# Attention scores in a hybrid decoder step: from two full-array products per head to three half-array products per head

## The chip, the cores and the metric

The kernel runs on one core of one Trainium2 chip. The metric is the device time of one execution in microseconds, given as the median of several runs. A profiled execution beside them gives the trace: every instruction on TensorE (PE; its weight loads are listed apart as PEld), VectorE (DVE), ScalarE (ACT), GpSimd (POOL) and the SyncE queue (SP) that issues the DMAs.

## The reference, cut to what matters

One layer of a hybrid decoder: 2048 prompt tokens and 8 sampled tokens, model width 1024. The input is normalised and projected into one wide vector whose columns feed three branches: attention with dilated windows, a gated linear recurrence, and cross-attention to a memory. The branches are gated, projected, merged and projected once more. The change touches the prompt's attention alone:

```python
A_WINDOWS = (128, 512, 2048)
A_DILATIONS = (1, 4, 16)
A_GROUPS = 3
A_HEADS = 8
A_HEAD_DIM = 64
...
    s = jnp.einsum('brnqhd,brnkhd->brnhqk', qb, kb) * (Dh ** -0.5)
...
    s = jnp.where(mask[None, None, :, None], s, -jnp.inf)
    m = jnp.max(s, axis=-1, keepdims=True)
    p = jnp.exp(s - m)
    l = jnp.sum(p, axis=-1, keepdims=True)
    o = jnp.einsum('brnhqk,brnkhd->brnqhd', p / l, vb)
    lse = (m + jnp.log(l))[..., 0].transpose(0, 1, 2, 4, 3)
```

There are three groups of eight heads of width 64. In each group the tokens are split into residue classes of the dilation, and 128 queries at a time read their own block of 128 keys and the block before it, where there is one. The result is wanted at nearly fp32 accuracy.

## The kernel before, in words

**Exact halves.** To keep nearly fp32 accuracy the kernel multiplies in the type float32r and splits each factor into a high part (a cast to float32r) and a low part (the rest). A product is then made of several products of parts. The projections use three: high by high, high by low, low by high (lines 402 to 404, and 163 to 165 elsewhere).

**Order of work.** TensorE's instructions keep the order in which the program issues them. A loop at the end of the kernel's second phase writes this order: `gate_stream` is the main stream (the last 24 units of the input projection, lines 402 to 404), and beside it run side streams. A side stream yields an estimated cost on TensorE and the least time until it is due again; when its time has come by this planned clock its next piece is issued, else the next piece of the projection. For the attention the gap is 3.0 us (`ATT_GAP`), and a step's scores are planned at 0.86 us. These numbers are the same before and after. While one attention step's results travel through the other engines, TensorE works on the projection. When the attention has ended, the recurrence follows as the next side stream, then the memory attention and the sampled tokens. The other engines' instructions are put in order by the framework, which also places the semaphores. The data's DMAs of this stretch are issued on the SP queue in turn.

**The attention stream** (`attention`) takes 96 steps: 4 pairs of heads, 3 groups, 8 segments of 256 queries. Three stages are in flight. One turn of the stream issues the weighted values of the step two back (line 611; evicted at line 614), the transposes of the weights of the step before (line 595; evicted at line 597), and the scores of the current step.

A step's scores cover two blocks (`b`) of 128 queries and two heads (`h`). A block has 256 key columns where there is a block before it, else 128; group 2 has only single blocks. Per block and head, VectorE adds the mask and takes the minimum of the negated scores (line 580), and ScalarE takes the exponential and its sum (line 582).

**The split before.** Queries of both heads are loaded twice, by two DMAs, so that each head's 64 dimensions lie on both halves of the 128 partitions (line 526; the key is loaded at line 528). VectorE casts the queries (`qh`, line 540, 512 columns), and makes per head a tile `km` whose one half holds the high part of the keys and whose other half holds the low part (lines 544 and 545, 64 partitions each, twice per step), then the low part of the queries (`ql`, line 546, 512 columns). With the contraction over 128 partitions, `qh` by `km` gives high by high plus high by low, and `ql` by `km` gives low by high plus low by low: two products per block and head (lines 575 and 576), eight in a step. `km` keeps the keys of two steps, for the block before.

**Banks.** The attention has five banks of the accumulator (PSUM): two for scores (one per block, holding both heads), two for transposes, one for values. The projection has three others.

**Merge.** When a pair of heads has finished its three groups, `merge` combines them by their sums; its work on VectorE (lines 693, 696, 700) and GpSimd (line 695) and its DMAs run during the next pair's steps. The gated projections' evictions (lines 479 to 497) use the same engines.

Of the kernel before, what the change touches and what calls it, by code (L numbers as in the profile page):

```python
# [10 lines left out]
F32 = mybir.dt.float32  # L11
F32R = mybir.dt.float32r
AF = mybir.ActivationFunctionType
ALU = mybir.AluOpType
# [29 lines left out]
class Region:  # L44
    """Rings of buffers, by tag, in parts (tile, from, to: KB) of on-chip tiles; what reuses a buffer waits for its last users only."""
# [23 lines left out]
class Banks:  # L69
    """Rings of PSUM banks, by tag."""  # L70
# [27 lines left out]
def tile_hybrid_step(ctx: ExitStack, tc: tile.TileContext, I: dict, O: dict):  # L98
# [68 lines left out]
    # ================= normalised inputs and the input projection =================  # L167
# [9 lines left out]
    def at_token(t0):  # L177
        """Chunk that holds the 128-token tile (or the sampled tokens) at t0, and its columns there."""
        i = max(i for i, (c0, _) in enumerate(CHUNKS) if c0 <= t0)
        return i, t0 - CHUNKS[i][0]  # L180

    class Weights:
        """A unit of 256 weight columns, brought in by pieces of 256 rows as exact high and low parts."""
# [24 lines left out]
    if True:  # L208
# [12 lines left out]
        class Prep:  # L221
            """Normalised columns c0.. of src as exact high and low parts."""
# [41 lines left out]
        class Values:  # L264
            """A unit of w_v: the values of the sampled tokens beside its weights, then the prompt's by token tile."""
# [119 lines left out]
    class Projector:  # L385
        """Feature-major products of the units of w_t; the weights of the next unit are prepared half a unit ahead."""
# [29 lines left out]
    # forget-gate lower bound: softmax over the depth axis, first row  # L416
# [45 lines left out]
    # order of the last 24 units of w_t: az, bq, bf, bz, cq, cz (2 each), merge gates (12)  # L462
# [38 lines left out]
    def until(u):  # L501
        """Nothing before the given unit of the gate stream has begun."""
        while progress[0] < u:
            yield 0.0, 1.0

    # Side streams yield (time on the tensor engine of what they issued, least time until their next issue).
    def attention(ap, pool, rnd8, spawn):
        """Unnormalised outputs to uT, minimum of -s/8 and sum to st [p, g, (m l), h, 16]; three stages in flight.
# [915 lines left out]
```

## Time and profile before

| | |
|---|---|
| time, median of 3 runs | 3179.41 us (3178.95 to 3179.91) |
| profiled execution, span from first to last instruction | 3169.3 us |
| attention's stretch (990 to 1675 us) | 685 us for 96 steps |
| TensorE busy in that stretch | 644.51 us |
| VectorE busy in that stretch | 491.91 us |
| ScalarE busy in that stretch | 349.32 us |

No time other than its span is listed for the profiled execution. In the rows of the trace a matmul's duration is modelled and overlaps the next one's, so a stream's pace is read from start to start. "Idle before" is the time in which the engine stood still just before the instruction, and the name behind the arrow is what ended it. "SPq" is the queue that issues DMAs. An instruction group is named by its line in the kernel, its engine, and the tiles it writes and reads.

### The profile page before, as it was taken

To read this page: it belongs to the slowest core of one execution; us is meant where nothing else is said; L and a number is where in the kernel's file an instruction comes from. 1 tells how busy PE (TensorE), PEld (TensorE's weight loads), DVE (VectorE), ACT (ScalarE), POOL (GpSimd) and SP (SyncE) were. 2 spreads that over 40 slices of the span, in tenths; PEclk is the share of its full clock that TensorE was granted. 3 is DMA by queue.
4 is the path that set the end of the run, shared out by engine and by line. 5 is a ranking of instruction groups with operands and counts; after the bars stand their busy time and mean duration, and the time that the engine had idled before them with its cause. 6 is when DMAs were issued, how large, how long until landed. Compare 5 with 4: busy or idle time off the path is not lost. (4 is left out here: it accounts for less than half of the span.)

```text
span 3169.3 us, 56318 instructions
## 1 busy us (share of the span) xinstructions
PE 3023.6 (95%) x21644; PEld 2768.5 (87%) x21644; DVE 1530.8 (48%) x3827; ACT 993.0 (31%) x2468; POOL 1021.2 (32%) x836
## 2 busy tenths in 40 slices
PE   6999999999999999999989999999998988999998
PEld 6999999999999987878878888888886778899986
DVE  8700002222224776777772277777757356233232
ACT  4412110000003654434552244444443433201222
POOL 4312126556663211111222231112125125634411
PEclk9999999999999999999989999999999999999999
DMA  4332222112123567767675323233246467665442
GB/s 137 103 97 88 72 78 75 68 67 80 67 80 111 134 168 188 170 170 191 166 170 153 108 88 97 84 99 98 89 127 180 116 164 216 199 175 176 156 146 95
DMA packets 383134, 400.11 MB, mean 126 GB/s; under 512 B 89416, under 2 KB 306120, under 8 KB 379536
## 3 DMA queue, kind: packets, MB, share of 16 engines
q1 hardware_dynamic: 382864, 396.50, 43.3%
q8 instruction: 170, 2.79, 0.4%
q14 instruction: 100, 0.82, 0.1%
HBM read 257.71 MB, written 138.67 MB: 125 GB/s over the span
## 5 line engine op out<-in xcount | busy, mean ns | idle before, releaser
L402 PE MATMUL bank<-rnd 128*128 128x384 f32 (+2 forms) x2880 | 1033.8, 359 | 13.8 <-ACT side L479 7.6
L404 PE MATMUL bank<-rnd 128*128 128x384 f32 (+2 forms) x2880 | 1010.1, 351 | 6.4 <-POOL rnd L201 6.4
L403 PE MATMUL bank<-rnd 128*128 128x384 f32 (+2 forms) x2880 | 1010.2, 351 | 0.0
L402 PEld LDWEIGHTS bank<-rnd 128*128 128x128 f32 x2880 | 550.3, 191 | 43.3 <-ACT side L479 7.9
L404 PEld LDWEIGHTS bank<-rnd 128*128 128x128 f32 x2880 | 548.3, 190 | 32.2 <-POOL rnd L201 7.6
L403 PEld LDWEIGHTS bank<-rnd 128*128 128x128 f32 x2880 | 549.6, 191 | 23.3 <-issue 1.9
L163 PE MATMUL bank<-rnd 128*128 128x256 f32 (+4 forms) x1648 | 532.4, 323 | 8.4 <-DVE raw L1249 4.2
L165 PE MATMUL bank<-rnd 128*128 128x256 f32 (+4 forms) x1648 | 529.2, 321 | 3.5 <-POOL rnd L248 3.4
L164 PE MATMUL bank<-rnd 128*128 128x256 f32 (+4 forms) x1648 | 529.5, 321 | 1.9 <-POOL rnd L1228 1.2
L201 POOL TENSOR_TENSOR rnd<-raw,rnd 128x512 fp32r<-128x512 f32 x172 | 227.7, 1331 | 557.2 <-ACT rnd L200 550.9
L163 PEld LDWEIGHTS bank<-rnd 128*128 128x128 f32 (+1 forms) x1648 | 313.4, 190 | 25.2 <-ACT rnd L1214 3.6
L165 PEld LDWEIGHTS bank<-rnd 128*128 128x128 f32 (+1 forms) x1648 | 313.4, 190 | 17.3 <-POOL rnd L248 4.6
L164 PEld LDWEIGHTS bank<-rnd 128*128 128x128 f32 (+1 forms) x1648 | 313.6, 190 | 15.4 <-POOL rnd L1228 1.5
L200 ACT CAST rnd<-raw 128x512 fp32r<-128x512 f32 x172 | 105.4, 618 | 647.5 <-PE bank L403 449.3
L450 DVE TENSOR_TENSOR raw<-bank,raw 128x384 f32<-128x384 f32 (+2 forms) x120 | 70.4, 586 | 444.1 <-POOL side L455 179.3
L582 ACT ACTIVATE raw<-raw 128x256 f32<-128x256 f32 (+1 forms) x384 | 173.2, 453 | 157.4 <-DVE raw L580 156.5
L695 POOL TENSOR_TENSOR side<-side 128x512 f32<-128x512 f32 x32 | 51.6, 1614 | 334.5 <-DMA side<-stC 271.1
L1249 DVE TENSOR_TENSOR raw<-raw,bank 128x412 f32<-128x412 f32 (+1 forms) x120 | 67.3, 580 | 169.2 <-PE bank L165 93.7
L495 ACT ACTIVATE side<-side 128x384 f32<-128x384 f32 (+2 forms) x120 | 65.4, 545 | 241.1 <-DVE side L494 235.0
L491 POOL TENSOR_TENSOR side<-side 128x384 f32<-128x384 f32 (+2 forms) x60 | 67.8, 1129 | 226.7 <-ACT side L490 205.4
L580 DVE CUSTOM_DVE_ANT_0 raw<-bank,c_amask 128x256 f32<-128x256 f32 (+1 forms) x384 | 119.6, 358 | 18.0 <-PE bank L576 8.3
L286 DVE COPY raw<-bank 8x64 f32<-8x64 f32 x32 | 7.0, 220 | 246.3 <-PE bank L281 245.5
(267 smaller groups left out, 4260.8 us busy)
## 6 DMA issues: line engine op xcount, KB each, us to landing
raw<-in_w_t SPq DMA_DIRECT2D x144, 256.0 KB
raw<-qT SPq DMA_DIRECT2D x192, 128.0 KB
raw<-sgT SPq DMA_DIRECT2D x96, 206.0 KB
sgT<-side SPq DMA_DIRECT2D x72, 192.0 KB
qT<-side SPq DMA_DIRECT2D x12, 1028.0 KB
out_kT<-side SPq DMA_DIRECT2D x12, 1028.0 KB
out_vN<-raw SPq DMA_DIRECT2D x96, 128.0 KB
raw<-out_vN SPq DMA_DIRECT2D x96, 128.0 KB
```

The lines of the kernel that those rows point to most:

```text
L163: T.matmul(out, lhsT=lh, rhs=rh, start=(i == 0), stop=False)
L164: T.matmul(out, lhsT=lh, rhs=rl, start=False, stop=False)
L165: T.matmul(out, lhsT=ll, rhs=rh, start=False, stop=(i == n - 1))
L200: A.copy(hi, raw)
L201: G.tensor_tensor(lo, raw, hi.bitcast(F32), op=ALU.subtract)
L402: T.matmul(ps[:, :w], lhsT=hi, rhs=xh[c][:, k, :], start=(k == 0), stop=False)
L403: T.matmul(ps[:, :w], lhsT=hi, rhs=xl[c][:, k, :], start=False, stop=False)
L404: T.matmul(ps[:, :w], lhsT=lo, rhs=xh[c][:, k, :], start=False, stop=(k == KT - 1))
L450: V.tensor_tensor(t1[:, :w], ps[:, :w], rc[:, c0:c0 + w], op=ALU.mult)
L491: G.tensor_tensor(ow, ow, ew, op=ALU.mult)
L580: V.tensor_tensor_reduce(sm[:, :w], s[:, h, :w], amask[:, m0:m0 + w], -0.125, 1.0e38, ALU.add, ALU.min, accum_out=nmc)
L582: A.activation(sm[:, :w], sm[:, :w], AF.Exp, scale=-1.0, bias=nmc, accum_out=sts[hp][:, g, 1, h, idx:idx + 1])
```

## The change

Queries are loaded once, by one DMA, with the two heads on the two halves of the partitions as the keys have them. Queries and keys are each split into a high and a low tile of 128 partitions by 256 columns, by four VectorE instructions in place of six. Per block and head the scores are three products over that head's 64 partitions only: high by high, high by low, low by high; low by low is left out. The heads alternate within each product, and each head has a bank of its own that holds both blocks, in place of a bank per block that holds both heads. All twelve products of a step are issued ahead of the minima. The text of comments is taken out as well, which leaves the line numbers nearly as they were.

```diff
-        qh = rnd8.tile([128, 2, 256], F32R, name="a_qh")
-        ql = rnd8.tile([128, 2, 256], F32R, name="a_ql")
-        km = rnd8.tile([128, 2, 4, 128], F32R, name="a_km")
+        qh = rnd8.tile([128, 256], F32R, name="a_qh")
+        ql = rnd8.tile([128, 256], F32R, name="a_ql")
+        kh = rnd8.tile([128, 4, 128], F32R, name="a_kh")
+        kl = rnd8.tile([128, 4, 128], F32R, name="a_kl")
...
-            q = pool.tile([128, 2, 256], F32, tag="q", name="a_q")
-            for half in range(2):
-                dma(q[64 * half:64 * half + 64], qT[g * 4 + hp].rearrange("(h d) t -> d h t", h=2)[:, :, pp])
+            q = pool.tile([128, 256], F32, tag="q", name="a_q")
+            dma(q, qT[g * 4 + hp, :, pp])
...
             V.tensor_copy(qh, q)
             kv = k.rearrange("p (b t) -> p b t", b=2)
-            for h in range(2):
-                hi, lo = slice(64 * h, 64 * h + 64), slice(64 - 64 * h, 128 - 64 * h)
-                V.tensor_copy(km[hi, h, sl, :], kv[hi])
-                V.tensor_tensor(km[lo, h, sl, :], kv[hi], km[hi, h, sl, :].bitcast(F32), op=ALU.subtract)
+            V.tensor_copy(kh[:, sl, :], kv)
+            V.tensor_tensor(kl[:, sl, :], kv, kh[:, sl, :].bitcast(F32), op=ALU.subtract)
             V.tensor_tensor(ql, q, qh.bitcast(F32), op=ALU.subtract)
...
-            out = []
+            out, todo = [], []
+            ss = [ap.tile([128, 2, 256], F32, tag=f"s{h}", name="a_s") for h in range(2)]
             for b in range(2):
...
-                s = ap.tile([128, 2, 256], F32, tag="s", name="a_s", bufs=2)
+                bb = slice(b * 128, b * 128 + 128)
+                for j, (x, y) in enumerate(((qh, kh), (qh, kl), (ql, kh))):
+                    for h in range(2):
+                        hr = slice(64 * h, 64 * h + 64)
+                        T.matmul(ss[h][:, b, :w].rearrange("p (b t) -> p b t", t=128), lhsT=x[hr, bb], rhs=y[hr, ks, :],
+                                 start=(j == 0), stop=(j == 2))
+                todo.append((b, idx, blocks, w, m0))
+            for b, idx, blocks, w, m0 in todo:
                 sms = []
-                for h in range(2):
-                    o = s[:, h, :w].rearrange("p (b t) -> p b t", t=128)
-                    bb = slice(b * 128, b * 128 + 128)
-                    T.matmul(o, lhsT=qh[:, h, bb], rhs=km[:, h, ks, :], start=True, stop=False)
-                    T.matmul(o, lhsT=ql[:, h, bb], rhs=km[:, h, ks, :], start=False, stop=True)
                 for h in range(2):
...
-                    V.tensor_tensor_reduce(sm[:, :w], s[:, h, :w], amask[:, m0:m0 + w], -0.125, 1.0e38,
+                    V.tensor_tensor_reduce(sm[:, :w], ss[h][:, b, :w], amask[:, m0:m0 + w], -0.125, 1.0e38,
                                            ALU.add, ALU.min, accum_out=nmc)
```

## The prediction

> **What bounds the kernel now.** I read the page first, then the table of stretches, the waits of the attention's stretch, and the order of time on TensorE.
>
> ```profile
> span 3169.3 us, 56318 instructions
> PE 3023.6 (95%) x21644; PEld 2768.5 (87%) x21644; DVE 1530.8 (48%) x3827; ACT 993.0 (31%) x2468; POOL 1021.2 (32%) x836
> PE   6999999999999999999989999999998988999998
> ```
>
> TensorE (PE) is busy in nearly every slice: the kernel is one long stream of matmuls in an order fixed beforehand. A microsecond taken out of that stream, or out of a stall in it, moves all that comes behind; one taken from another engine counts only where TensorE waits. The profiled execution's span is 3169.3 us, and the median of the runs is 3179.41: 10.1 us lie around the span, and I carry them over unchanged.
>
> ```profile
> core 0: us, PE busy (x) PEld busy (x) DVE busy (x) ACT busy (x) POOL busy (x), PEclk, DMA share, GB/s
> 990.00:1675.00 685.00, 644.51 (x4434) 565.53 (x4433) 491.91 (x1586) 349.32 (x1126) 125.81 (x94) 0.97 0.65 167
> ```
>
> The attention's 96 steps lie in this stretch, 685/96 = 7.1 us each. TensorE stands idle for 685.00 - 644.51 = 40.5 us, and its granted clock is 0.97, which costs up to 0.03 x 685 = 21 us more. VectorE (DVE) is at 491.91/685 = 72%.
>
> ```profile
> ACT raw L582 <- DVE raw L580: 156.5, 81, 6.5
> PEld bank L595 <- ACT raw L582: 38.8, 81, 4.1
> DVE r L544 <- DMA raw<-out_kT: 25.3, 7, 7.0
> PE bank L595 <- ACT raw L582: 17.9, 20, 3.9
> PEld bank L576 <- DVE r L546: 10.9, 16, 2.9
> PE bank L576 <- DVE r L546: 8.2, 14, 2.7
> PEld bank L575 <- DVE r L545: 7.2, 17, 1.5
> PE bank L575 <- DVE r L545: 3.4, 4, 1.3
> PE bank L611 <- ACT raw L597: 4.1, 4, 2.1
> ```
>
> (Columns: total us, times, longest.) Two waits hold TensorE. The score products (L575, L576) wait for VectorE's split of q and k: 3.4 + 8.2 = 11.6 us by the matmul rows, 7.2 + 10.9 = 18.1 by the weight loads. The transposes (L595) wait for the exponentials, 17.9 us by the matmuls, 38.8 by the loads, and those wait for VectorE's masked minimum (L580, 156.5 us). Both waits lead to VectorE.
>
> **The score products.** Now eight full matmuls a step, each with a 128-column weight load; then twelve of 64 rows, in pairs on the two halves of the rows.
>
> ```profile
> 1516.66 0.28 PE L576 MATMUL bank<-r 128*128 128x256 f32 x1
> ...
> 1517.49 0.34 PE L402 MATMUL bank<-rnd 128*128 128x384 f32 x1
> ```
> ```profile
> 1492.32 0.28 PE L576 MATMUL bank<-r 128*128 128x128 f32 x1
> ...
> 1493.10 0.45 PE L402 MATMUL bank<-rnd 128*128 128x512 f32 x1
> ```
> ```profile
> L575 PE MATMUL bank<-r 128*128 128x256 f32 x216 | 61.5, 313 | 1.5 <-DVE r L545 1.3
> L575 PE MATMUL bank<-r 128*128 128x128 f32 x168 | 45.4, 300 | 2.8 <-DVE r L545 2.1
> ```
>
> Durations overlap, so I count pitch, start to start. Seven products of 256 columns take 0.83 us, 0.119 each; seven of 128 columns 0.78 us, 0.111 each. L576 runs as often as L575, so now 432 x 0.119 + 336 x 0.111 = 88.7 us. There are 108 wide and 84 narrow blocks, with three pairs each. If a pair takes the pitch of one matmul: 324 x 0.119 + 252 x 0.111 = 66.5 us, 22.2 less. If the twelve follow one another: 133.0 us, 44.3 more. Half the columns cost almost the same pitch, so the weight load sets it, and the question is whether the two heads' loads run side by side. No row has 64-row operands; the nearest ones split the array by columns:
>
> ```profile
> 1813.39 0.76 PE L757 MATMUL bank<-raw 128*32 128x32 f32 x64
> 1814.08 0.44 PE L402 MATMUL bank<-rnd 128*128 128x384 f32 x1
> ```
> ```profile
> 1836.09 0.34 PE L404 MATMUL bank<-rnd 128*128 128x384 f32 x1
> 1836.35 0.68 PE L788 MATMUL bank<-raw 128*64 128x64 f32 x8
> 1836.96 0.44 PE L402 MATMUL bank<-rnd 128*128 128x384 f32 x1
> 1837.24 0.34 PE L403 MATMUL bank<-rnd 128*128 128x384 f32 x1
> 1837.42 0.34 PE L404 MATMUL bank<-rnd 128*128 128x384 f32 x1
> ```
>
> L757 goes round four column strips: 64 products with their loads in 0.69 us, 0.011 each. L788 stays on one strip: eight in 0.61 us, 0.076 each, with twice the columns. So strips compute and load side by side, and I take the pair at one pitch, -22.2 us; the other end is +44.3.
>
> The Trainium skill, "TensorE: Matmul & The Clock Gate", section "LDWEIGHTS (loading the stationary operand)", speaks against the change: a load takes about its columns over 1.2 GHz whatever its rows, an estimated 107 ns for 128 columns, so half the rows save nothing; the 0.111 pitch agrees. By that figure 1152 loads in place of 768 add 41 us if they queue.
>
> **Going in and out of the half-array.** L404 to L788 takes 0.26 us where 0.18 is usual (L403 to L404): 0.08 to empty the array. Behind the strips L402 to L403 takes 0.28: 0.10 because the first load had no matmul to hide behind. I count 0.18 to 0.20 for each passage, so 0.2 us into the scores (from the transposes, full-array today) and 0.2 out: 0.4 x 96 = 38.4 us. The lower end is nothing, if halving rows is no passage; a gain has no ground. I take 38.4, since the column strips show it. Where the scores wait for VectorE anyway, part hides under that wait.
>
> The Trainium skill, "TensorEngine Tiling (Array Packing)", section "Key Properties", says that a change of tiling mode drains TensorE; the 0.26 agrees, for column strips, and no row here shows it for rows; by that rule the rival without passages falls away.
>
> Pairs and passages make +16.2 us in TensorE's stream.
>
> **The split on VectorE.**
>
> ```profile
> L545 DVE TENSOR_TENSOR r<-raw,r 64x256 fp32r<-64x256 f32 x192 | 91.5, 476 | 5.9
> L546 DVE TENSOR_TENSOR r<-raw,r 128x512 fp32r<-128x512 f32 x96 | 70.1, 730 | 2.0
> L544 DVE CAST r<-raw 64x256 fp32r<-64x256 f32 x192 | 66.3, 345 | 44.8 <-DMA raw<-out_kT 25.3 <-PE bank L576 14.7 <-DMA side<-uT 1.7
> L540 DVE CAST r<-raw 128x512 fp32r<-128x512 f32 x96 | 42.6, 444 | 5.5 <-POOL side L458 5.5
> ```
>
> Now 0.444 + 2 x 0.345 + 2 x 0.476 + 0.730 = 2.82 us a step. Then two casts and two subtractions of 128x256. The 64x256 rows have as many elements per partition, so I take 2 x 0.345 + 2 x 0.476 = 1.64; half of the 128x512 rows would give 1.17. So 1.18 us a step are saved (to 1.65), 113 us of VectorE's 492.
>
> It has more effect than its own wait: in narrow steps the split lies between the minima that the exponentials wait for.
>
> ```profile
> 1650.30 0.28 DVE L580 CUSTOM_DVE_ANT_0 raw<-bank,c_amask 128x128 f32<-128x128 f32 x1
> ...
> 1653.23 0.29 DVE L580 CUSTOM_DVE_ANT_0 raw<-bank,c_amask 128x128 f32<-128x128 f32 x1
> ```
>
> Between these two minima of one step stand 2.9 us, most of them the split. I take 16 us of the scores' wait (11.6 to 18.1: a wait averages 0.85 us at L575 and 0.6 at L576, less than is saved), 15 of the transposes' (nothing to 38.8; many follow a merge or a late k, which a shorter split doesn't mend), 2 of the 4.1 at L611, and 5 of the 21 us of clock (nothing to 21): 38 us. The bounds are 12 (the scores' alone) and 82.
>
> **The banks.** Before, a block's two heads share a bank, and the first minimum may start after four of eight matmuls. Then a bank holds both blocks of one head, and if a whole bank is waited for, all minima queue behind the twelfth. That is 6 x 0.119 + 0.2 - 4 x 0.119 = 0.44 us later, while the score stage grows by 0.71 + 0.4 - 0.95 = 0.16: the chain to the transposes loses 0.28 us. Who waits is ScalarE's exponentials, then the transposes. It costs in steps in which the transposes wait, 20 by the matmul row, 81 by the loads: 5.6 to 22.7 us. I take 5.6. The next scores need both banks free, so all four minima; on VectorE's queue their split stands behind most of these already, so I cost that at nothing. Should the split run ahead of them, it costs what is left of the minima, some 0.3 us.
>
> **Loads.**
>
> ```profile
> raw<-qT SPq DMA_DIRECT2D x188, 128.0 KB
> ```
> ```profile
> 1198.27 0.59 SPq L526 DMA_DIRECT2D raw<-qT  x1
> ```
>
> Of two q loads a step one goes: 96 x 128 KB = 12.6 MB less, and 96 x 0.59 = 57 us of issuing on SP's queue, which also carries k, v, the merge's and the weights' loads. These come earlier. The row to measure it by is VectorE's 25.3 us for k: I take 4 us, between nothing and 10.
>
> **Sum.** +16.2 - 38 + 5.6 - 4 = -20.2 us; 3179.4 - 20.2 = 3159.2. By bounds: passages half hidden, relief 60 and loads 10 give -57; relief 16 and the banks' 22.7 give +23.
>
> **Rivals.**
>
> *The halves take turns.* The pair's loads queue, so the pitch holds per matmul: +44.3 + 38.4 - 38 - 4 + 5.4 (the banks, 1.15 later against 0.88 grown, in 20 steps) = +46, or 3225.5. It decides from the point where 1152 p + 38.4 - 88.7 exceeds the 36.4 that split and loads give net of the banks (38 + 4 - 5.6): p = 0.075 us per matmul. For it speaks that the pitch is the load's and that the strips seen had narrow loads; against it the 0.011 of L757.
>
> *No passage.* Halving the rows empties nothing. Then -22.2 - 38 - 4, and the banks' chain loses 0.24 + 0.24 = 0.48 in 20 steps, +9.6: -54.6, or 3124.8. For it: no row shows a passage for rows. Against it: every narrow group in the trace pays.
>
> *No halves at all.* The instructions run as full-array matmuls with half the rows empty: +44.3 with no passages, -38 - 4, and the banks' 8 x 0.119 - 4 x 0.119 = 0.48 net in 20 steps, +9.5: +11.8, or 3191. Nothing in the trace speaks for it except that such operands do not occur.
>
> **How the numbers follow.** The sum as costed has 0.50, the halves taking turns 0.24, no passage 0.20, no halves 0.06. A measurement of this kernel tells about 0.2%, 6.4 us, from no change. In the first case I see 0.36 faster, 0.09 within, 0.05 slower; no passage is faster, taking turns slower, no halves 0.04 slower and 0.02 within. So faster 0.56, within 0.11, slower 0.33. The likeliest case's own range is 3122 to 3202; with the rivals, 3115 to 3226.
>
> **What would show it.** Score rows with 64 rows, 576 for each head: two starts within some 0.02 us and the next pair 0.12 later confirm the pairs; an even 0.11 is the rival. The first projection pitch behind the scores at 0.28 confirms the passage, 0.17 denies it. VectorE's split should fall from 271 to some 157 us, its whole to about 1418; DMA by 12.6 MB; the waits at the split below 3 us, the exponentials' at L595 by a third. I am wrong in mechanism if the waits stay though VectorE is lighter, for then merges and loads, not the split, held TensorE; or if the split rows of 128x256 take over 0.6 us.

## The result and the profile after

The changed kernel takes 3152.59 us, the median of 4 runs (3151.64 to 3163.23); the kernel before, on the same chip, 3179.18 (3178.40 to 3179.91). The ratio is 0.9922, with an interval of 0.9905 to 0.9938: 24.8 us faster by the ratio, 26.6 by the medians. The forecast was 20.2 us faster (3159.2, range 3115 to 3226).

The page of the changed kernel, its first lines:

```profile
span 3149.9 us, 56777 instructions
PE 3017.3 (96%) x22028; PEld 2746.6 (87%) x22028; DVE 1402.9 (45%) x3635; ACT 995.7 (32%) x2468; POOL 1020.5 (32%) x836
PE   6999999999999999999899999999998988999998
```

This profiled execution took 3151.64 us, so 1.7 us lie around its span, and about as much in every other run here. The 10.1 us that I carried over are therefore not there: with 1.7 us around it, the execution profiled before would have taken 3169.3 + 1.7 = 3171.0 us, some 8 us less than the median of its kernel. The two spans differ by 19.4 us, and what follows is about these; the other 5 to 7 us lie between executions of the kernel before, and no trace shows them.

VectorE is 127.9 us lighter (1530.8 to 1402.9; the split accounts for 116 of them), and the DMA queues moved 387.54 MB in place of 400.11, which is the 12.6 MB of query loads.

The stretch of the attention, by the same window as before:

```profile
core 0: us, PE busy (x) PEld busy (x) DVE busy (x) ACT busy (x) POOL busy (x), PEclk, DMA share, GB/s
990.00:1675.00 685.00, 659.86 (x4934) 561.08 (x4933) 371.54 (x1407) 356.61 (x1142) 126.24 (x97) 0.97 0.56 153
```

TensorE is idle for 685.00 - 659.86 = 25.1 us in place of 40.5, though the attention also ends 20 us sooner. The waits of that stretch (total us, times, longest):

```profile
ACT raw L583 <- DVE raw L581: 152.3, 85, 6.4
DVE r L540 <- PE bank L573: 39.0, 39, 1.4
PEld bank L596 <- ACT raw L583: 33.2, 62, 4.6
DVE r L542 <- PE bank L573: 26.2, 25, 1.7
PE bank L596 <- ACT raw L583: 17.4, 12, 4.3
```

The transposes (L596) wait as long as before by the matmul rows, 17.4 us against 17.9, and little less by the weight loads, 33.2 against 38.8. Of the two waits that I expected to shrink, this one has not. What has gone are the score products' waits for the split, as the groups of the score products and of the split show:

```profile
L573 PE MATMUL bank<-r 64*128 64x256 f32 x648 | 57.6, 306 | 2.0 <-DVE r L544 1.4 <-DVE r L540 0.6
L573 PE MATMUL bank<-r 64*128 64x128 f32 x504 | 40.4, 287 | 0.0
L544 DVE TENSOR_TENSOR r<-raw,r 128x256 fp32r<-128x256 f32 x96 | 47.5, 494 | 0.6
L543 DVE TENSOR_TENSOR r<-raw,r 128x256 fp32r<-128x256 f32 x96 | 42.9, 447 | 2.5
L540 DVE CAST r<-raw 128x256 fp32r<-128x256 f32 x96 | 33.8, 352 | 48.0 <-PE bank L573 39.0 <-POOL side L458 5.4 <-DMA raw<-qT 2.6
L542 DVE CAST r<-raw 128x256 fp32r<-128x256 f32 x96 | 30.2, 314 | 27.3 <-PE bank L573 26.2 <-DMA raw<-out_vN 1.2
```

The scores now wait 2.0 us (11.6 before). The split takes 47.5 + 42.9 + 33.8 + 30.2 = 154.4 us. One wait has grown: the next step's cast (L540, L542) waits on VectorE's queue for the score products that still read the tile that it writes, 39.0 + 26.2 us, where 14.7 us stood before (L544), and the step's minima stand behind it.

TensorE's order of time around one step's scores, with the pair's pace and the passage out:

```profile
1199.07 1.01 PE L573 MATMUL bank<-r 64*128 64x256 f32 x12
1200.01 0.44 PE L402 MATMUL bank<-rnd 128*128 128x384 f32 x1
1200.29 0.33 PE L403 MATMUL bank<-rnd 128*128 128x384 f32 x1
1200.46 0.34 PE L404 MATMUL bank<-rnd 128*128 128x384 f32 x1
```

Twelve products of 64 rows are done in 0.94 us from the first start to the next work; twelve at a pitch of 0.119 would take 1.43. The single starts in the trace are 0, 4, 223, 225, 341, 345, 460, 465, 581, 585, 698, 705 ns: the two heads start together, and the pairs follow at some 0.119. L402 to L403 takes 0.28 where L403 to L404 takes 0.17.

### Where the time went: step by step

An average over the stretch hides what happened, so I took the starts of the first score product of all 96 steps and set the steps apart: wide ones (groups 0 and 1, 64 steps) and narrow ones (group 2, 32 steps). The table of stretches, cut at these starts for group 2 of each of the four pairs of heads, before:

```profile
1102.01:1151.39 49.38, 47.66 (x330) 41.92 (x329) 36.54 (x127) 28.41 (x100) 11.78 (x9) 1.00 0.71 171
1273.04:1326.02 52.98, 48.30 (x324) 41.16 (x323) 36.68 (x130) 23.06 (x90) 7.12 (x5) 1.00 0.80 184
1446.06:1497.67 51.61, 49.81 (x317) 42.81 (x317) 39.25 (x136) 21.26 (x84) 6.80 (x5) 0.93 0.79 189
1621.28:1671.82 50.54, 46.58 (x285) 41.89 (x284) 34.58 (x116) 27.10 (x93) 11.58 (x10) 0.87 0.65 157
```

and after:

```profile
1102.16:1149.40 47.24, 47.24 (x360) 40.84 (x359) 24.98 (x108) 27.45 (x100) 10.53 (x9) 1.00 0.59 157
1270.26:1316.99 46.73, 46.73 (x355) 39.91 (x354) 21.04 (x105) 23.13 (x90) 5.03 (x4) 1.00 0.55 159
1434.22:1480.61 46.39, 46.39 (x348) 39.04 (x347) 24.11 (x111) 21.05 (x85) 5.04 (x4) 1.00 0.56 154
1610.79:1651.65 40.86, 40.86 (x312) 35.22 (x311) 21.34 (x94) 25.41 (x91) 7.78 (x8) 1.00 0.42 118
```

(The last stretch ends at the start of the last step.) Group 2 takes 181.2 us in place of 204.5: 23.3 us less, more than the whole difference of the spans. Before, TensorE is idle in it for 1.7 + 4.7 + 1.8 + 4.0 = 12.2 us, and its granted clock of 0.93 and 0.87 costs 0.07 x 51.61 + 0.13 x 50.54 = 10.2 us. After, it is never idle and never slowed. The sums over groups 0 and 1 of the same tables, before and after:

```profile
sum 470.44, PE 442.11 PEld 387.79 DVE 338.93 ACT 245.43 POOL 85.18; mean PE 110.53 PEld 96.95 DVE 84.73 ACT 61.36 POOL 21.30
```
```profile
sum 473.61, PE 448.53 PEld 378.52 DVE 273.31 ACT 248.21 POOL 91.39; mean PE 112.13 PEld 94.63 DVE 68.33 ACT 62.05 POOL 22.85
```

The wide steps, two thirds of all, became 3.2 us slower although VectorE does 66 us less in them.

The gain is not spread over the narrow steps either. Beside the first pair of heads, where no merge runs, the median narrow step went from 5.78 to 5.86 us and the median wide one from 6.57 to 6.66: an ordinary step is 0.08 to 0.09 us slower. But before, ten narrow steps took over 1 us longer than the median of their kind, 26.0 us in excess of it together; after, none does. Among the wide steps there were 18 such late ones with 45.8 us in excess, and there are 16 with 45.8 us. **The change is a small loss in every step, and a gain in ten steps that came late.**

One of the ten, VectorE's order of time before:

```profile
1642.07 0.29 DVE L580 CUSTOM_DVE_ANT_0 raw<-bank,c_amask 128x128 f32<-128x128 f32 x1 [0.49 <-ACT side L488]
...
1649.55 0.28 DVE L544 CAST r<-raw 64x256 fp32r<-64x256 f32 x1 [6.97 <-DMA raw<-out_kT]
1649.76 0.41 DVE L540 CAST r<-raw 128x512 fp32r<-128x512 f32 x1
1650.09 0.28 DVE L580 CUSTOM_DVE_ANT_0 raw<-bank,c_amask 128x128 f32<-128x128 f32 x1
```

and TensorE's:

```profile
1646.62 0.44 PE L595 MATMUL bank<-ident,raw 128*128 128x128 f32 x2
1650.96 0.86 PE L595 MATMUL bank<-ident,raw 128*128 128x128 f32 x2 [3.91 <-ACT raw L582]
...
1655.25 0.52 PE L402 MATMUL bank<-rnd 128*128 128x384 f32 x1
1655.57 0.52 PE L403 MATMUL bank<-rnd 128*128 128x384 f32 x1
```

The minima of the step's first block are done at 1642.6. Those of its second block stand on VectorE's queue behind a cast for the next step, and the cast waits 6.97 us for a key that is still on its way. TensorE gets its last two transposes 3.91 us late, and the projection then runs at 0.32 us from start to start in place of 0.17, because the clock fell; between 1651 and 1655 us the granted clock was 0.53. This step took 10.19 us and the next one 8.80: over the median of 5.78 one late key cost 4.4 + 3.0 us. The Trainium skill, "TensorE: Matmul & The Clock Gate", section "What's actually happening", says that an idle window of about 3.4 us halves the clock; the 3.91 us and the 0.53 agree. But the clock of this trace falls after shorter waits too: in the wide step at 1437.6 us TensorE stands idle for 1.17 us in all, and the step behind it runs at a granted clock of 0.64.

Late keys are not what all ten have in common. By the trace they are of four kinds; the excess is over the median narrow step, 5.81 us over all four pairs of heads:

| step starts at, us | it took, us | what the trace shows | excess, us |
|---|---|---|---|
| 1108.2, 1292.5, 1299.4, 1641.3 | 8.30, 6.84, 7.15, 10.19 | the split on VectorE waits 5.02, 3.66, 3.27 and 6.97 us for a key | 9.2 |
| 1651.5 | 8.80 | clock of 0.62 behind the step above | 3.0 |
| 1306.5, 1484.5 | 8.26, 7.67 | ScalarE waits 4.14 and 2.90 us for weights of the projection | 4.3 |
| 1446.1, 1621.3 | 9.53, 9.36 | clock of 0.64 and 0.68 behind a late wide step | 7.3 |
| 1273.0 | 8.02 | VectorE is busy for 7.69 us; the split and the merge stand ahead of the minima | 2.2 |

Keys thus account for 12.2 of the 26.0 us at most, with the slow clock behind one of them. In the two steps of ScalarE no minimum is late. A cast of projection weights (L200) stands there between the exponentials of the two blocks and waits for its load:

```profile
1313.26 0.62 ACT L200 CAST rnd<-raw 128x512 fp32r<-128x512 f32 x1 [4.14 <-DMA raw<-in_w_t]
1313.79 0.40 ACT L582 ACTIVATE raw<-raw 128x128 f32<-128x128 f32 x1
```
```profile
1314.33 0.71 PE L595 MATMUL bank<-ident,raw 128*128 128x128 f32 x2 [2.02 <-ACT raw L582]
```

The minima of that block were done at 1309.5 us. Before, such a cast lies between the two blocks' exponentials in four of the 32 narrow steps; after the change nothing does.

### The profile page after: what moved, and what is told of

Same layout as the page of the kernel before. It is cut to its first block, busy times and chain, and to the rows that moved or that the text cites. A ratio compares the mean times of both kernels' runs of the same rounds, so it can differ in the third digit from the quotient of the medians.

```text
span 3149.9 us, 56777 instructions
## 1 busy us (share of the span) xinstructions
PE 3017.3 (96%) x22028; PEld 2746.6 (87%) x22028; DVE 1402.9 (45%) x3635; ACT 995.7 (32%) x2468; POOL 1020.5 (32%) x836
## 2 busy tenths in 40 slices
DMA packets 369311, 387.54 MB, mean 123 GB/s; under 512 B 87881, under 2 KB 292297, under 8 KB 365713
## 5 line engine op out<-in xcount | busy, mean ns | idle before, releaser
L402 PE MATMUL bank<-rnd 128*128 128x384 f32 (+2 forms) x2880 | 1041.4, 362 | 14.7 <-DVE side L494 8.4
L404 PE MATMUL bank<-rnd 128*128 128x384 f32 (+2 forms) x2880 | 1009.1, 350 | 4.6 <-POOL rnd L201 4.6
L403 PE MATMUL bank<-rnd 128*128 128x384 f32 (+2 forms) x2880 | 1009.2, 350 | 0.0
L402 PEld LDWEIGHTS bank<-rnd 128*128 128x128 f32 x2880 | 548.7, 191 | 55.0 <-DVE side L494 9.4
L404 PEld LDWEIGHTS bank<-rnd 128*128 128x128 f32 x2880 | 547.8, 190 | 30.2 <-POOL rnd L201 5.5
L403 PEld LDWEIGHTS bank<-rnd 128*128 128x128 f32 x2880 | 548.8, 191 | 23.1 <-issue 1.9
L163 PEld LDWEIGHTS bank<-rnd 128*128 128x128 f32 (+1 forms) x1648 | 312.6, 190 | 25.1 <-issue 4.2
L200 ACT CAST rnd<-raw 128x512 fp32r<-128x512 f32 x172 | 106.1, 619 | 631.8 <-PE bank L403 453.8
L1254 POOL TENSOR_TENSOR raw<-raw 128x412 f32<-128x412 f32 (+1 forms) x80 | 89.8, 1123 | 96.2 <-DVE raw L1250 90.1
L598 ACT COPY raw<-bank 128x256 f32<-128x256 f32 (+1 forms) x192 | 87.2, 492 | 101.1 <-PE bank L596 99.3
```

The lines of the kernel that those rows point to most:

```text
L163: T.matmul(out, lhsT=lh, rhs=rh, start=(i == 0), stop=False)
L200: A.copy(hi, raw)
L402: T.matmul(ps[:, :w], lhsT=hi, rhs=xh[c][:, k, :], start=(k == 0), stop=False)
L403: T.matmul(ps[:, :w], lhsT=hi, rhs=xl[c][:, k, :], start=False, stop=False)
L404: T.matmul(ps[:, :w], lhsT=lo, rhs=xh[c][:, k, :], start=False, stop=(k == KT - 1))
L598: A.copy(pts[:, :, :nb, :], pt[:, :, :nb, :])
```

## The theories

*Length.* The shorter split frees VectorE, as predicted; the order of its work does not matter. *Order.* With a bank per head all four minima of a step become ready together, so the split no longer gets between them: before, two casts of the next step lie between the blocks' minima in 28 of 32 narrow steps; after, in none, since they stand ahead of all four. *Late loads.* What makes a step late is a split that waits for its load with minima queued behind it; before it waited 25.3 us for keys, after some 5 us for all loads. (The table above shows that this covers about half of the late steps' excess.) *Halves in turn* is the prediction's strongest rival. All figures by group are worked out as above, from the starts of the first score products.

## The experiments

**The changed kernel again**, measured beside three of the runs below: the split as long but behind its useful part, the kernel before with a shorter split, and two query loads both used.

> The changed kernel unaltered, to have it on the same chip as the three beside it: ratio to the kernel before 0.990 to 0.994.

It took 3148.38 us against 3176.07, ratio 0.9921 (0.9905 to 0.9938). Group 2 takes 181.1 us, the wide steps 471.3, with 18 late ones.

**A split as long as before, ahead of the minima** (e1).

```diff
+            V.tensor_copy(d1, q)
+            V.tensor_copy(d2, k)
+            V.tensor_tensor(d1, q, d2.bitcast(F32), op=ALU.subtract)
             V.tensor_tensor(ql, q, qh.bitcast(F32), op=ALU.subtract)
```

> The changed kernel with two more casts and one more subtraction of 128x256 per step on VectorE, whose results nobody reads: the split costs VectorE again what it cost before (some 2.8 us a step), all else is as changed. If the gain comes from the shorter split, it goes: TensorE's stream alone is some 15 us longer than before (pairs -22, passages in and out of the half-array +37), so 3185 to 3200 us, and the transposes' and scores' waits return. Rival, the gain lies in TensorE's pairs or in the fewer loads: 3150 to 3165, hardly moved.

3201.59 us, ratio 1.0087 (1.0072 to 1.0102), 29 us slower than before. The time lies near the 3185 to 3200 us that the theory of the length gave, but the length is not what this shows. The waits from 985 to 1690 us:

```profile
DVE r L546 <- DMA raw<-qT: 138.9, 70, 5.4
```

The added cast was placed ahead of the minima, and it waited there for queries that had not arrived, 70 times. Nine narrow steps are late again (26.8 us), and group 2 takes 208.4 us. This is what the late key does, now in most steps: a split that waits for a load while the minima stand behind it.

**The two heads one after the other.**

```diff
-                for j, (x, y) in enumerate(((qh, kh), (qh, kl), (ql, kh))):
-                    for h in range(2):
+            for h in range(2):
+                for b, idx, blocks, w, m0, ks in todo:
+                    for j, (x, y) in enumerate(((qh, kh), (qh, kl), (ql, kh))):
```

> The changed kernel with one head's six products ahead of the other's six, so that only one pair can overlap. If the halves work side by side in the changed kernel, eleven pitches replace six: 0.55 to 0.6 us a step, 50 to 55 us more on TensorE's stream, less a few because the first head's minima may start earlier: 3190 to 3205 us. Rival, the order in which they are issued does not matter (TensorE pulls the other half's products forward): 3150 to 3160.

3160.94 us, ratio 0.9964 (0.9951 to 0.9976): by the ratios 0.0043 of 3170, 13.6 us more than the changed kernel, which was not measured beside it; still faster than before. In a narrow step:

```profile
1120.45 1.17 PE L575 MATMUL bank<-r 64*128 64x128 f32 x12
1121.55 0.45 PE L402 MATMUL bank<-rnd 128*128 128x384 f32 x1
```

The twelve take 1.10 us. The sum from the first to the last score start grew from 68.8 to 99.4 us over all steps, so alternating the heads is worth 30.6 us of TensorE's stream, not the 50 to 55 forecast. But the first head's minima start sooner (1.11 us behind the first score's start in place of 1.34, medians), late wide steps fall to 11 with 30.0 us in excess of their own, longer median, and from the first step's start to the last's it takes 11.2 us more only.

**The kernel before, with a part of its split on other engines.**

```diff
-            V.tensor_copy(qh, q)
+            A.copy(qh, q)
...
-            V.tensor_tensor(ql, q, qh.bitcast(F32), op=ALU.subtract)
+            G.tensor_tensor(ql, q, qh.bitcast(F32), op=ALU.subtract)
```

> The kernel before with its full-array products and its two q loads, but the queries' cast on ScalarE and their low part on GpSimd: VectorE's split falls by 0.444 + 0.730 = 1.17 us a step, as much as in the change. If the shorter split is what pays, this gains without the passages: 3135 to 3155 us, some 10 us better than the changed kernel, less what ScalarE (0.6 us more a step) delays the exponentials. Rival, the half-array products are needed for the gain: 3170 to 3185.

3174.43 us, ratio 1.0012 (1.0001 to 1.0023): no gain. A good part of the relief did not come about, because VectorE's own part became slower:

```profile
L546 POOL TENSOR_TENSOR r<-raw,r 128x512 fp32r<-128x512 f32 x96 | 129.3, 1347 | 212.4 <-ACT r L540 181.8 <-DMA raw<-out_kT 10.9 <-DMA raw<-qT 5.2
L545 DVE TENSOR_TENSOR r<-raw,r 64x256 fp32r<-64x256 f32 x192 | 116.8, 608 | 6.1
L544 DVE CAST r<-raw 64x256 fp32r<-64x256 f32 x192 | 88.8, 462 | 38.4 <-PE bank L576 19.7 <-DMA raw<-out_kT 9.7 <-POOL side L458 5.5
```

The casts went from 345 to 462 ns and the subtractions from 476 to 608, which gives back 47.8 us of the 112.7 taken away. Nine narrow steps stay late. The other 65 us did leave VectorE, but the split now also waits on ScalarE and GpSimd for its loads, so the run doesn't test the length by itself.

**The changed kernel, with the queries loaded twice** (e4; the second copy unused).

```diff
+            q2 = pool.tile([128, 256], F32, tag="q2", name="a_q2")
+            dma(q2, qT[g * 4 + hp, :, pp])
```

> The changed kernel with every q block loaded a second time into a buffer that nobody reads: the SP queue and the DMA engines carry as much as before. The prediction put 4 us on these loads (nothing to 10): 3153 to 3163 us, most likely 3156. Rival, the relief of the loads is the main gain: 3170 or more.

3173.17 us, ratio 1.0002 (0.9992 to 1.0012): the whole gain is gone, but with a wait that the kernel before does not have. On the queue that issues the DMAs:

```profile
SPq L528 <- DMA raw<-qT: 51.4, 56, 2.1
```

The unused copy has no reader, so its buffer is free only when the copy two steps back has landed, and the queue stood 56 times for that, the key's load behind it. So it tells nothing of the price of the loads as such; the split waited 29.8 us for late ones. Most of the loss, 14.0 us, lies in the wide steps (487.6 us in place of 473.6).

**A split as long, behind its useful part.** The three added instructions read what the split has made, not what was loaded.

```diff
+            V.tensor_copy(d1, qh.bitcast(F32))
+            V.tensor_copy(d2, kl[:, sl, :].rearrange("p b t -> p (b t)").bitcast(F32))
+            V.tensor_tensor(d1, qh.bitcast(F32), d2.bitcast(F32), op=ALU.subtract)
```

> As e1, but the two casts and the subtraction read the split's own results, so that they stand inside the split, as the old instructions did, and hold no load's buffer: VectorE's split is as long as before. If the shorter split is what pays, 25 to 40 us are lost against the changed kernel: ratio to the kernel before 1.000 to 1.005. Rival, e1 lost its 49 us because its extra casts stood ahead of the minima and waited for q's load (138.9 us there): ratio 0.993 to 0.996.

3152.78 us, ratio 0.9935 (0.9919 to 0.9950). The split lasts 258 us, nearly the 270 of before, and group 2 takes 181.1 us as without it. Load on VectorE as such costs nothing in the narrow steps and some 4 us by the ratio in all, within the intervals.

**The kernel before, with a shorter split.** The queries' low part is made once and the second head's low keys in the first two steps only.

```diff
-                V.tensor_tensor(km[lo, h, sl, :], kv[hi], km[hi, h, sl, :].bitcast(F32), op=ALU.subtract)
-            V.tensor_tensor(ql, q, qh.bitcast(F32), op=ALU.subtract)
+                if h == 0 or i < 2:
+                    V.tensor_tensor(km[lo, h, sl, :], kv[hi], km[hi, h, sl, :].bitcast(F32), op=ALU.subtract)
+            if i == 0:
+                V.tensor_tensor(ql, q, qh.bitcast(F32), op=ALU.subtract)
```

> The kernel before, but the low part of the queries is made in the first step only and the low part of the second head's keys in the first two steps only (later steps multiply by those): VectorE's split is 0.73 + 0.48 = 1.21 us shorter, as in the change, with full-array products, both q loads and no work on another engine. If the shorter split pays by itself: 20 to 35 us, ratio 0.989 to 0.994. Rival, the loads pay: at most 8 us, ratio 0.997 or more.

3146.25 us, ratio 0.9913 (0.9895 to 0.9931). With the products, banks and loads of before, a split cut by 112 us gives 28 us, as much as the whole change and as the theory of the length had it. It comes from other places, though: the wide steps fall from 470.4 to 454.6 us, group 2 only to 193.5, with seven late steps. The split's wait for keys halves to 12.7 us.

**The changed kernel, with two query loads a step, both used** (the low part is made from the second copy).

```diff
-            q = pool.tile([128, 256], F32, tag="q", name="a_q")
-            dma(q, qT[g * 4 + hp, :, pp])
+            q = pool.tile([128, 2, 256], F32, tag="q", name="a_q")
+            for half in range(2):
+                dma(q[:, half, :], qT[g * 4 + hp, :, pp])
```

> The changed kernel with two q loads of 128 KB a step into one tile with two halves, the second read by the subtraction in place of the first: bytes, issues and buffer waits as before, VectorE's work as changed. e4 put 20 us on the second load, but its SP queue also waited 51.4 us for the landing of q itself. If the loads are worth 20 us, ratio to the kernel before 0.998 to 1.001; if that wait was e4's own, the 4 us of the prediction: 0.992 to 0.995.

3151.72 us, ratio 0.9932 (0.9915 to 0.9948): 3.5 us over the changed kernel by the ratios, which the intervals do not tell from nothing. Group 2 stays at 181.1 us.

**The kernel before, minima first.** The split is issued only behind the fourth minimum of the step before.

```diff
-            split(i)
+            with tc.issue_after(last[0].ins):
+                split(i)
```

> The kernel before, with one thing changed: each step's split of queries and keys stands behind the fourth minimum of the step before it on VectorE's queue. Nothing is left out; the split is as long as before (some 270 us), products, banks and loads are those of before. Theory (the order on VectorE in the narrow steps of group 2 is the gain): group 2 falls from 204.5 us to 180 to 188, the last of a narrow step's four minima ends 1.0 to 1.3 us behind the last score product (before 1.98 median), and the time is 0.989 to 0.995 of before. Rival (the length of the split, the banks by head or the half-array products make the gain): group 2 stays over 198 and the ratio is 0.998 to 1.003. Second rival (the split comes too late for the next scores when it waits for all minima): group 2 falls, but groups 0 and 1 grow by more than 10 us together and the ratio is over 0.998.

3159.49 us, ratio 0.9963 (0.9953 to 0.9973): 11.7 us, half of the gain. Group 2 falls to 195.7 us, the wide steps to 464.9. None of the three expectations had this. The last of a narrow step's minima ends 0.65 us behind the last score product (1.98 before, medians), so the minima are no longer held; the waits show what came in their place:

```profile
PEld bank L581 <- DVE r L547: 25.9, 28, 2.8
PE bank L581 <- DVE r L547: 20.8, 24, 2.6
```

The score products (here L581) now wait 20.8 us for the split's last instruction, 8.2 before. The order moves the wait from the transposes (17.9 us before, 4.7 now) to the scores. The split's length by itself does not explain that: in the changed form one of 258 us kept group 2 at 181.1. Six narrow steps are late.

**The changed kernel, with casts between the minima** of the narrow steps, as before.

```diff
+                    if g == 2 and b == 0 and h == 1 and i + 1 < len(steps):
+                        with tc.issue_after(r.ins):
+                            after = casts(i + 1)
```

> The changed kernel, with one thing changed back: in the narrow steps of group 2 the next step's two casts stand between the minima of the first and of the second block on VectorE, as the split did before. Nothing is left out and no work is added. Theory (the order is the gain): the last minimum of a narrow step ends 0.6 to 0.9 us later than in the changed kernel, group 2 grows from 181 to 195 to 206 us, groups 0 and 1 stay within 3, and the time is 0.996 to 1.001 of the kernel before. Rival (the order does not matter, the shorter split or the half-array products are the gain): group 2 stays below 186 and the ratio at 0.991 to 0.994.

3149.96 us, ratio 0.9941 (0.9928 to 0.9953), beside the next run on one chip. VectorE's order of time shows that the edit took effect:

```profile
1639.57 0.29 DVE L591 CUSTOM_DVE_ANT_0 raw<-bank,c_amask 128x128 f32<-128x128 f32 x1
1639.78 0.08 DVE L591 DVE_READ_ACCUMULATOR2_ANT raw<- 128x1 f32 x1
1639.78 0.29 DVE L541 CAST r<-raw 128x256 fp32r<-128x256 f32 x1
1639.98 0.28 DVE L543 CAST r<-raw 128x256 fp32r<-128x256 f32 x1
1640.18 0.28 DVE L591 CUSTOM_DVE_ANT_0 raw<-bank,c_amask 128x128 f32<-128x128 f32 x1
```

Group 2 takes 181.1 us, not a tenth more. The last minimum of a narrow step ends 0.40 us later than in the changed kernel, less than the 0.6 to 0.9 that the theory named and than the 0.91 between the two kernels. So much delay costs nothing: the last exponential still ends 2.6 us (median) ahead of its last transpose. The theory of the order falls as far as the delay by the casts themselves is concerned; no load was late behind the casts here.

**The changed kernel, minima first in all steps.** The edit is that of the kernel before with minima first.

> The changed kernel, with each step's split placed behind the fourth minimum of the step before it in all steps, the wide ones too, where in the changed kernel a cast stands ahead of the minima. Nothing is left out. Theory (any split ahead of the minima delays the transposes' wait): in wide steps the first minimum starts 0.3 to 0.5 us sooner behind the last score product, groups 0 and 1 fall by 5 to 20 us together, and the time is 0.985 to 0.991 of before. Rival (the split's start, not the minima, holds the wide steps: it is then late for the next scores): groups 0 and 1 stay or grow, ratio 0.992 to 0.997.

3143.47 us, ratio 0.9920 (0.9906 to 0.9934). In the wide steps the first minimum starts 0.14 us behind the last score product in place of 0.53, and these steps take 467.6 us. The rival had said that they would stay or grow. It is 6.5 us faster than the run with casts between the minima on the same chip, but by its ratio no better than the changed kernel (0.9922 and 0.9921). No version here beats the change by more than a measurement can tell.

**The kernel before, with keys a step earlier.** A third buffer for the keys; to make room the merge's joint weights share a buffer of another ring.

```diff
+            k = pool.tile([128, 256], F32, tag="k", name="a_k", bufs=3)
+            dma(k, kT[g * 4 + hp, :, pp])
...
                 load(i + 2)
+            if i + 3 < len(steps):
+                load_keys(i + 3)
```

> The kernel before, with one thing changed: the keys have a third buffer and are loaded three steps ahead in place of two, so that a key load is issued one step (some 6 to 7 us) sooner. To make room the merge keeps its joint weights in a buffer of its ring for weights. Nothing is left out; split, its order, products, banks and query loads are those of before. Theory (a late key, for which the split waits on VectorE with a block's minima queued behind it, makes the late narrow steps): the split's wait for keys falls from 25.3 us to under 5, of the ten steps of group 2 that take over 6.8 us at most four remain, group 2 falls from 204.5 us to 183 to 192, and the time is 0.992 to 0.997 of before. Rival (the length of the split on VectorE's queue makes them late, the wait for keys only fills time): the wait for keys vanishes, but group 2 stays over 198 us and the ratio over 0.998. Second rival (the queries come as late as the keys did): the wait turns up at the queries' cast with over 10 us, and group 2 stays over 198.

3165.01 us, ratio 0.9985 (0.9974 to 0.9997). The keys are issued 22.5 us ahead of their first product in group 2 (15.9 before, medians), and the split's wait for them is gone. This is what stands there now:

```profile
DVE r L545 <- DMA raw<-qT: 13.3, 5, 3.8
```

The queries' cast, L545 here, waits 13.3 us: the second rival. Group 2 falls by 4.0 us to 200.5, with nine late steps. The step shown above lost its 7 us of key wait and took 6.94 us in place of 10.19; the one at 1108 us went from 8.30 to 5.72.

### All kernels side by side

Ordered by the time that the split waits for DMAs in the attention's stretch (the moved split with ScalarE's and GpSimd's waits); "late" is over 1 us above the median of its kind.

| kernel | split waits for loads, us | late narrow steps | group 2, us | groups 0 and 1, us | ratio |
|---|---|---|---|---|---|
| changed, minima first | 0 | 0 | 181.1 | 467.6 | 0.9920 |
| changed, again | 2.1 | 0 | 181.1 | 471.3 | 0.9921 |
| changed, casts between minima | 2.6 | 0 | 181.1 | 472.0 | 0.9941 |
| changed, split as long, behind | 2.6 | 0 | 181.1 | 472.1 | 0.9935 |
| changed, heads in turn | 4.4 | 0 | 189.6 | 476.4 | 0.9964 |
| changed | 4.7 | 0 | 181.2 | 473.6 | 0.9922 |
| changed, two query loads | 6.9 | 0 | 181.1 | 476.3 | 0.9932 |
| before, minima first | 8.1 | 6 | 195.7 | 464.9 | 0.9963 |
| before, split cut | 12.7 | 7 | 193.5 | 454.6 | 0.9913 |
| before, keys early | 13.3 | 9 | 200.5 | 470.9 | 0.9985 |
| before | 27.0 | 10 | 204.5 | 470.4 | 1 |
| changed, queries twice | 29.8 | 3 | 188.2 | 487.6 | 1.0002 |
| before, split moved | 41.4 | 9 | 203.0 | 474.0 | 1.0012 |
| changed, split as long, ahead | 170.8 | 9 | 208.4 | 491.6 | 1.0087 |

Where the split waits for up to 6.9 us, no narrow step is late; where it waits longer, some are. That is weak evidence. The boundary is read off the table itself, and all rows above it are of the changed form and all but two below it of the form before, so any other difference between the two forms divides the rows nearly as well. Step by step, the split's loads are not the whole cause. In the run with early keys the five steps that late keys had cost 12.2 us fell to an excess of 2.9, but ScalarE's waits for weights, 4.76 and 3.31 us, and the slow clock behind them brought four others from 3.7 to 9.4. In the run with the split cut, one of the seven late steps holds a wait of the split for its load (2.35 us), and four hold ScalarE's for weights (3.08 to 4.59 us). What the late steps share more widely is an engine that takes its work in order and stands before a load, or is full, with minima or exponentials behind; no run takes all of that out of the kernel before. Nor do keys that are issued sooner tell the forms apart: in group 2 they go out 15.9 us ahead of their first product before and 18.7 after (medians), but 14.1 with minima first in the changed kernel, where no narrow step is late.

Within the changed form each part can be undone by itself (length, order, query loads) and group 2 stays at 181.1; put into the kernel before by itself, each gives only a part: minima first 8.8 us of group 2's 23.3, a shorter split 11.0, early keys 4.0. The half-array products and the bank per head were not put into the kernel before by themselves. The margin of the narrow steps is made by several parts together, and their shares are not settled.

## Why the prediction came out right, point by point

**Pairs and passages: right in kind, about half in sum.** Pairs run side by side, at the pitch of one matmul. From the last transpose to the first score the start-to-start time went from 0.03 to 0.20 us, from the last score to the projection from 0.11 to 0.20, and the first projection pitch from 0.18 to 0.28: 0.36 a step with a first pair that takes some 0.05 to 0.1 longer, where I took 0.4. The Trainium skill, "TensorEngine Tiling (Array Packing)", section "Key Properties", has both, that a change of mode drains TensorE and that tiles work independently of each other; these starts agree for rows. Together I forecast +16.2 us in the stream; the ordinary step's 0.08 and 0.09 us make 32 x 0.08 + 64 x 0.09 = 8.3, an estimate that also holds whatever else an ordinary step gained.

**The split: right.** 154.4 us against some 157; VectorE 1402.9 against 1418, with 12 us of the fall outside the split.

**The relief of 38 us: too large, and in the wrong place.** This is the step that failed: "in narrow steps the split lies between the minima that the exponentials wait for". The rows that I quoted for it, at 1650.30 and 1653.23, belong to two steps; within one step two casts lie between the minima, and casts put back there cost nothing. Where a cast waited long for a load, as at 1641 us, it was the load and not the split's length that held the minima. By terms: the scores' wait fell by 9.6 us (11.6 to 2.0) for my 16. The transposes' fell by 0.5 for my 15; the trace's start-to-start sums show why. From transpose to transpose it is 13.3 us less in narrow steps, and from the values to the transposes 9.9 us more in wide ones. The clock's 5 us are right for the wrong reason: the narrow steps got back 10.2, and since the stretch as a whole stays at 0.97, the wide steps gave about half of it away (0.92 in the last pair's, from 1480.61 to 1610.79 us, where 0.97 stood before). Against an ordinary step's loss of 8.3 and a span 19.4 us shorter, the relief of all kinds is 27.7 us. That the forecast came out near is luck in part: the relief was some 10 us smaller than I took it and the stream's loss some 8 us smaller, and most of the relief came in ten late steps that the sum did not know of. The lower bound was also added wrongly: passages half hidden, relief 60, banks 5.6 and loads 10 make -67, not -57.

**The banks: not told apart.** No narrow transposes wait, so it costs nothing there. In wide steps the run with heads in turn, whose first minima come 0.23 us sooner, has 15.8 us less of late steps than the changed kernel, though over a median that is 0.26 us longer; the forecast of 5.6 to 22.7 may hold. What I set aside in the same place, "should the split run ahead of them, it costs what is left of the minima, some 0.3 us", did happen: casts went ahead of the minima. Without that the wide steps are 6.0 us shorter (473.6 to 467.6), which the time does not confirm; two profiles of the changed kernel itself differ there by 2.3 us.

**Loads: not told from nothing.** Forecast 4 us, 3.5 by the run with two used query loads. I weighed them as an average over the stretch and saw 25.3 us of VectorE's time; a late load's price lies in the few steps in which minima or exponentials stood behind it, and the second query load did not bring these back.

**The rivals.** The starts 4 ns apart rule out that the halves take turns, and the passages seen rule out the other two. Issued head by head, the twelve still overlap in part: 13.6 us, where the rival's price was 66 above the forecast.

**What should have shown me wrong** was in the text: "if the waits stay though VectorE is lighter, for then merges and loads, not the split, held TensorE". In the wide steps that is what happened: 45.8 us of late steps before and after, all beside the second to fourth pair of heads, where merges run.

## What to carry to other kernels

Before you spread a wait over a stretch, cut the stretch into its steps and look at how long each takes: here a wait of 18 us in 96 steps was 20 single waits, and the question is what made those steps late. Then go through the late steps one by one, since they need not share a cause. On every engine that takes its work in order, look for the instruction that waits for a DMA and for what stands behind it; here a TensorE wait of 3.9 us cost 7.4, the rest as a slow clock behind it. Making the engine lighter is then not the same as taking the waiting instruction out of the way: the minima first gave half of the gain with no work saved, and a split cut by 112 us left ScalarE's waits for weights standing in four late steps.

## What the runs showed of the hardware that I had not expected

Two 64-row products on the two halves start 2 to 7 ns apart, each with its own 128-column weight load. With a part of the split on GpSimd, VectorE's casts became 34% slower (345 to 462 ns) and its subtractions 28% (476 to 608). It is the overlap in time that counts: a cast beside GpSimd's subtraction took 836 ns on average, one beside no GpSimd instruction 287. The Trainium skill, "GPSIMD Engine Reference", section "1. Specifications", says that GpSimd shares its SBUF interfaces with VectorE, with contention in two-port modes or with two inputs; the subtractions agree in kind, and for the casts, which have one input, no row shows the mode. And a TensorE wait of 3.91 us was followed by 9 us at a granted clock of 0.53 (four of them) and 0.69 (five).
